# Seven-product steps in the mix and down products of a decoder block: one more in each, eleven premade sums, and activation sums made later

## The chip, the cores and the metric

One Trainium2 chip, one core. The metric is the device time of one execution in microseconds, the median of several runs. Times inside an execution come from a hardware profile of one run: its span, the busy time of each engine (PE is TensorE's matmuls, PEld its weight loads, DVE VectorE, ACT ScalarE, POOL GpSimd, SP SyncE), who waited for whom, and timelines.

## The reference

One decoder layer in float32 over 256 positions of width 2048. A large input projection, attention in three dilated groups and a gated recurrence end in gated branches y. Then, and this is the part that the change touches:

```python
h = h + rmsnorm(y @ w_mix_out[layer], norm_mix_post[layer])
a = rmsnorm(h, norm_ffn_pre[layer])
gt, up = jnp.split(a @ w_ffn_gate_up[layer], [D_FF], axis=-1)
ff = (jax.nn.silu(gt) * up) @ w_ffn_down[layer]
h = h + rmsnorm(ff, norm_ffn_post[layer])
```

`w_mix_out` is 2048 x 2048, `w_ffn_gate_up` 2048 x 11264, `w_ffn_down` 5632 x 2048. The weights are read once, 432 MB of traffic in all.

## The kernel before

**Split numbers.** Each float32 operand is split into a high part that TensorE multiplies exactly (ScalarE casts it, w or dh, L389 and L414) and the rest (VectorE subtracts, wl or dl, L409 and L417). A product takes three matmuls: high by high, high by low, low by high.

**Wide steps.** The large products run in blocks of 1024 output columns (two groups of 512), class `Wide`. A step takes 256 rows of the weight: two row blocks by two column groups, for two sides of 128 positions. By eight products that is 8 x 3 = 24 matmuls of 512 columns. By seven (in Strassen's manner) it is 21. For this a seven needs
- sums of the weight's four quarters (d, 128 x 1536; L399 to L404), split into dh and dl,
- one of them in the raw tile itself: after the raw load a DMA of GpSimd's queue adds the second row block onto the first (L302), so that the tile's high and low parts wait for it too,
- sums of the activations, split as well (so; `seven_sums`, from L543): in the mix by `pair_sums` (L555) in one of two lanes of side work, in the down product by `prep_act` within the step,
- four PSUM banks p1, p5, p6, p7, which after a block's last seven are gathered (L519 to L528) and then added to the four banks of the block's results (`add_up`, L533).

**Order of the work.** The instructions stand on each engine in program order. The main loop works two steps ahead: `ahead(n)` casts step n+2, makes its sums and its wl, and splits the sums of step n+1. There are three tiles for w, three for wl, one each for dh and dl. Three raw tiles (four from the FFN on): the load of step n+3 (n+4) waits until wl of step n is done. Where a block's last step is a seven, the gathering, `add_up` and only then wl of the step after next follow each other (`late`).

**The mix** is two blocks of eight steps, given by `MIX` as (row pair, by seven). In the first block, steps 3 and 5 are sevens, in the second, steps 2 and 4. The activations' sums of yT, pairs 0 and 1, are made in one go when pair 1 is there (`sums_of_y`, L1198). Beside its steps ScalarE's queue loads gains and x (gpost, hx, L1228 and L1235). Then `from_mix_to_ffn` interleaves the last steps, the norm and the first FFN steps by hand.

**The down product** is two blocks of 22 steps, `DOWN`; 8 steps of the first are sevens, and 9 of the second. The last three steps are run by side and column group, with the final norm behind them.

**Premade sums.** For steps listed in `READY` (by block and step: blocks 2 to 10 of the FFN, 11 and 12 for the two down blocks) the sums d are made ahead in DRAM, by six DMAs of GpSimd's queue each: three plain ones (L445), then, each on the one before, three accumulating ones (L449). Generators in `sums_before` are advanced once per step in the query-key-value stage, with `PACE` (4 steps between parts, 6 between starts). When a seven's sums are split, SyncE's queue loads the premade sums of the second next seven (`get_ready`, L423), in front of later raw loads. Such a step makes no additions for d.

Of the kernel before, what the change touches and what calls it, by code (L numbers as in the profile page):

```python
# [24 lines left out]
KF = FF // P  # L25
# [8 lines left out]
COL_GA, COL_GB = 13312, 15360  # L34

X7, H7 = tuple(range(4)), tuple(range(5))
MIX = [[(3, 0), (4, 0), (5, 0), (0, 1), (6, 0), (1, 1), (2, 0), (7, 0)],
       [(3, 0), (4, 0), (0, 1), (5, 0), (1, 1), (2, 0), (6, 0), (7, 0)]]

def order(steps):  # L40

    k = steps.count("7")
    return [(steps[:i].count(x) + k * (x == "8"), int(x == "7")) for i, x in enumerate(steps)]
# [1 line left out]

EARLY = [order(x) for x in ["88878878"] + ["87878787"] * 6 + ["88787878"]]
FFN = [order(x) for x in ["88878787"] + ["87877877", "87877877", "87877877", "87877877", "87877877", "87877877", "87877877", "87877877", "87877877"]]
DOWN = [[((n + 16 * j) % 22, n in by7) for n in range(KF // 2)] for j, by7 in enumerate( ([4, 6, 8, 10, 12, 14, 16, 18], [1, 3, 5, 7, 9, 11, 13, 15, 17]))]

TURN = 1  # L50
PAIRS = ((0, 0), (0, 1)), ((1, 0), (1, 1)), ("p1", "p6"), ("p5", "p7")
# [2 lines left out]


N_F = 16
READY, PACE, FIRST_READY, LAST_READY = {(2, 1), (2, 3), (3, 1), (3, 3), (4, 1), (4, 3), (5, 1), (5, 3), (6, 1), (6, 3), (7, 1), (7, 3), (8, 1), (8, 3), (9, 1), (9, 3), (10, 1), (10, 3), (11, 6), (11, 10), (11, 14), (12, 3), (12, 7), (12, 11), (12, 15)}, (4, 6), 2, 85


class Block:  # L60
# [48 lines left out]
def tile_hybrid_block(ctx: ExitStack, tc: tile.TileContext, t, out):  # L109
# [12 lines left out]
    def nm(s):  # L122
        serial[0] += 1
        return f"{s}_{serial[0]}"

    def rslot(s):
        return rpool.tile([P, 1024], F32R, tag="r", bufs=16, name=nm(s))
# [30 lines left out]
    def p3(s, dtype, n, bufs, tag=None):  # L158
        return pool["now"].tile([P, n], dtype, tag=tag or s, bufs=bufs, name=nm(s))
# [4 lines left out]
    def small(s, n=8, bufs=6):  # L164
        return cpool.tile([P, n], F32, tag=f"small{n}", bufs=bufs, name=nm(s))
# [65 lines left out]
    def ptile(s):  # L231
        n = {"early": 4, "middle": 5, "late": 2}[pool["name"]]
        return pool["now"].tile([P, 512], F32, tag="p", bufs=n, name=nm(s))
# [9 lines left out]
    blocks, seq, units, extra = [], [], [], []  # L243
# [11 lines left out]
    def add_seven(*args, flip, whole=True, stage=None, **kw):  # L255
        b = Wide(*args, **kw)
        b.flip, b.whole, b.unit0, b.stage = flip, whole, len(units), stage
        b.plus = stage == "ffn"
        blocks.append(b)
        for i in range(b.steps):  # L260
            seq.append(Step(b, i, len(units), 0))
            units.append([seq[-1]])
# [118 lines left out]
    def split_wide(st):  # L381

        b, raw = st.block, st.raw
        m, by7 = b.order[st.i]
        prep = b.prep(m, by7) if b.prep else iter(())
        next(prep, None)
        hi, lo = wslot(), wlow()
        st.parts = hi, lo
        nc.scalar.activation(hi, raw, AF.Copy)  # L389
        yield  # L390
        next(prep, None)
        if by7:
            w = raw.rearrange("p (n c) -> p n c", n=4)
            flat = st.sums
            if st.ready is None:
                flat = sums_slot(st)
                d = flat.rearrange("p (n c) -> p n c", n=3)
                if b.plus:
                    nc.vector.tensor_add(d[:, 0], w[:, 0], w[:, 2])  # L399
                    nc.vector.tensor_sub(d[:, 1], d[:, 0], w[:, 1])  # L400
                    nc.vector.tensor_add(d[:, 2], d[:, 0], w[:, 3])
                else:
                    nc.vector.tensor_sub(d[:, 0], w[:, 0], w[:, 2])
                    nc.vector.tensor_sub(  # L404
                        d[:, 1:], w[:, 1:4:2], d[:, 0:1].to_broadcast([P, 2, 512])
                    )
            st.rest = split_sums(st, flat, prep)
        yield
        nc.vector.tensor_sub(lo, raw, hi.bitcast(F32))  # L409

    def split_sums(st, flat, prep):

        hi, lo = (p3(x, F32R, 1536, 1) for x in ("dh", "dl"))
        nc.scalar.activation(hi, flat, AF.Copy)  # L414
        yield
        next(prep, None)
        nc.vector.tensor_sub(lo, flat, hi.bitcast(F32))  # L417
        st.parts += hi, lo
        later = [x for x in seq[st.n + 1 :] if type(x.block) is Wide and x.block.order[x.i][1]]
        if len(later) > 1 and later[1].ready is not None:  # L420
            get_ready(later[1])

    def get_ready(st):  # L423

        st.sums = sums_slot(st)
        nc.sync.dma_start(st.sums, st.ready)

    def sums_slot(st):
        n = [x for x in seq if x.block.__class__ is Wide and x.block.stage and x.block.order[x.i][1]]
        if len(H7) < 5 or st not in n:  # L430
            return p3("sum", F32, 1536, 1)
        return p3(("sum", "sum2")[n.index(st) % 2], F32, 1536, 1)
# [110 lines left out]
    def seven_sums(f, dst):  # L543

        s = ptile("s").rearrange("p (n t) -> p n t", n=4)
        x = f.rearrange("p k (s t) -> p (k s) t", s=2)
        nc.vector.tensor_sub(s[:, :2, :], x[:, 0:4:3, :], x[:, 1:2, :].to_broadcast([P, 2, P]))
        nc.vector.tensor_add(s[:, 2, :], s[:, 1, :], x[:, 0, :])
        nc.vector.tensor_sub(s[:, 3, :], x[:, 2, :], s[:, 2, :])
        yield  # L550
        nc.scalar.activation(dst[:, 0], s, AF.Copy)
        yield
        nc.vector.tensor_sub(dst[:, 1], s, dst[:, 0].bitcast(F32))

    def pair_sums(x, which, store, slot):  # L555

        for m in which:
            f = ptile("f").rearrange("p (k t) -> p k t", k=2)
            xs = x.slots[m]
            nc.vector.tensor_add(f, xs[:, :, 0, :].bitcast(F32), xs[:, :, 1, :].bitcast(F32))  # L560
            dst = slot().rearrange("p (z n t) -> p z n t", z=2, n=4)
            yield from seven_sums(f, dst)
            store[m] = sums_of(dst)
            yield

    def sums_of(dst):
        return lambda n: (dst[:, 0, n, :], dst[:, 1, n, :])
# [107 lines left out]
    evacs, turns, lanes, work, done = deque(), deque(), [deque(), deque()], deque(), []  # L675
# [16 lines left out]
    def flush(q):  # L692
        q = deque(q) if type(q) is list else q
        while q:
            advance(q)
# [477 lines left out]
    yT = []  # L1173
# [22 lines left out]
        return go  # L1196

    def sums_of_y():  # L1198
        while 1 not in yT[0].there:
            yield  # L1200
        yield from pair_sums(yT[0], (0, 1), y7, lambda: rslot("so"))


    zg, hx, gpost, zss = {}, {}, [], []
    h_t, hT, y7 = {}, [], {}
# [5 lines left out]
    def begin_mix():  # L1211
        flush(evacs)
        nc.scalar.preload_act_table_set("natural_log_exp_and_others")
        zss.append(small("zss"))

    def beside_mix(i):

        if i == 0:
            advance(turns)
        elif i == 1:  # L1220
            flush(turns)
        elif i < 4:
            j = i - 2
            if len(H7) > 4:
                gpost.append(p3("gpost", F32, (1024, 1536)[j], 1, ("act", "sum2")[j])[:, :1024])
            else:
                gpost.append(p3("gpost", F32, 1024, 3, "act"))
            nc.scalar.dma_start(  # L1228
                gpost[j],
                t["norm_mix_post"][:, j * 1024 : (j + 1) * 1024].to_broadcast([P, 1024]),  # L1230
            )
        else:
            j = i - 4
            hx[j] = p3("hx", F32, 1024, 4, "so").rearrange("p (b c) -> p b c", b=2)
            nc.scalar.dma_start(hx[j], xv[:, :, j * 512 : (j + 1) * 512])  # L1235
# [392 lines left out]
    for j in range(4):  # L1628
        add("N", t["w_attn_branch"][0], 8, 512 * j, heads, evac_attn_branch(j))
    blocks[-2].pre = lambda: lanes[1].append(sums_of_y())  # L1630
    blocks[-1].at[2] = begin_late
    for j in range(2):
        add_seven(t["w_mix_out"][0], (1024 * j, 1024 * j + 512), MIX[j],
                  lambda k: yT[0].after(turns)(k), lambda m: y7[m], evac_mix, flip=j == 0, whole=False,
                  pre=None if j else begin_mix, post=None if j else beside_mix)
    mix_end = len(seq) - 2
    mix_last = len(blocks) - 1
# [8 lines left out]
    for j in range(2):  # L1646
        add_seven(t["w_ffn_down"][0], (1024 * j, 1024 * j + 512), DOWN[j], act,
                  lambda m: a7[m], evac_down, stage="down", prep=prep_act, flip=j == 1, whole=j == 0,
# [3 lines left out]

    for n, st in enumerate(seq):
        st.n = n
    for j, b in enumerate(blocks[mix_last + 3 :], 1):
        b.plus = any(k == j for k, _ in READY)
    ready_in = range(blocks[10].unit0 + FIRST_READY, blocks[10].unit0 + LAST_READY)
    before = sums_before([
# [12 lines left out]
    later = []  # L1671
# [41 lines left out]
    for n, st in enumerate(seq):  # L1713
        b, i = st.block, st.i
# [49 lines left out]
    a, b, c = seq[-3:]  # L1764
# [61 lines left out]
```

## Time and profile before

| | us |
|---|---|
| runs before | 1686.75, 1684.83, 1686.53; median 1686.53 |
| the profiled execution | 1685.28 |
| its span | 1683.1 |
| TensorE busy | 1671.8 (99%) |
| VectorE busy | 1427.2 (85%) |
| ScalarE busy | 938.5 (56%) |
| mix, from the first to the last matmul of its 16 steps | about 900 to 985 |
| down product, 44 steps | about 1445 to 1674 |

The profile gives the span in forty slices, the groups of instructions by line and shape (count, busy time, mean duration, idle time in front of them and what ended it), who waited for whom, the chain of work that ended last, and timelines (start, duration, what; in brackets the idle time in front of it and its releaser). Matmuls are pipelined: they follow each other faster than the duration of one. TensorE's granted clock is full in nearly all slices.

### The profile page before, as it was taken

The numbers are of one execution on the slowest core, as the hardware profiler recorded it, in microseconds if no ns is written. First come the engines' busy times: TensorE is split into PE (matmuls) and PEld (weight loads), VectorE is DVE, ScalarE is ACT, GpSimd is POOL, SyncE is SP. The second block draws the span as 40 slices with busy tenths as digits, with TensorE's granted clock in tenths as the row PEclk, the third lists the DMA queues.
The fourth block names the chain that finished last, engine by engine and source line by source line (L and its number), as shares of the span: only waits on it lengthen the run. The fifth ranks groups of instructions, "written<-read, shape, count | busy, mean of one in ns | idle before, by whom it ended". The sixth has DMA issues, their size and how long they took to land.

```text
span 1683.1 us, 21771 instructions
## 1 busy us (share of the span) xinstructions
PE 1671.8 (99%) x8181; PEld 1402.6 (83%) x8181; DVE 1427.2 (85%) x1505; ACT 938.5 (56%) x962; POOL 225.2 (13%) x310
## 2 busy tenths in 40 slices
PE   9999999999999999999999999999999999999997
PEld 7888888888888888888888888888888888888886
DVE  6888898985887986777668887999999999899998
ACT  6655555554535434544445565566666666666763
POOL 0111111002320331321200010111111111000010
PEclk9999999999999999999999999999999999999999
DMA  8788888778995997995948857998998998888892
GB/s 280 264 264 253 260 260 257 244 244 290 319 265 175 318 292 232 303 313 177 291 150 250 269 174 253 276 273 273 277 273 271 277 287 265 263 256 253 242 301 99
DMA packets 241737, 432.63 MB, mean 257 GB/s; under 512 B 15168, under 2 KB 81776, under 8 KB 241632
## 3 DMA queue, kind: packets, MB, share of 16 engines
q1 hardware_dynamic: 201808, 337.55, 59.5%
q0 software_dynamic: 37200, 87.77, 22.5%
q10 hardware_dynamic: 2624, 5.92, 1.1%
q8 instruction: 64, 1.05, 0.3%
q14 instruction: 41, 0.34, 0.1%
HBM read 418.08 MB, written 52.43 MB: 280 GB/s over the span
## 4 chain that ended last, share of the span: by engine, by line
PE 94%; DVE 3%; issue 1%; DMA 1%; ACT 1%; SPq 0%; DVEq 0%; ACTq 0%
PE acc L168 59%; PE aux L168 34%; DVE wl L409 1%; DMA raw<-in_w_in 1%; PE aux L963 0%; PE acc L1451 0%; DVE dl L417 0%; PE aux L1451 0%; PE aux L632 0%; DVE e L537 0%; DVE w L355 0%; PE aux L620 0%; DVE e L528 0%; DVE fz L1573 0%; ACT w L354 0%
## 5 line engine op out<-in xcount | busy, mean ns | idle before, releaser
L389 ACT ACTIVATE w<-raw 128x2048 fp32r<-128x2048 f32 x204 | 390.2, 1913 | 220.8 <-issue 76.4
L409 DVE TENSOR_TENSOR wl<-raw,w 128x2048 fp32r<-128x2048 f32 x204 | 465.2, 2287 | 20.9 <-ACT w L389 19.0
L168 PE MATMUL acc<-xT,w 128*128 128x256 f32 (+1 forms) x2048 | 369.8, 339 | 0.0
L168 PEld LDWEIGHTS acc<-xT,w 128*128 128x128 f32 x2048 | 312.0, 188 | 43.8
L355 DVE TENSOR_TENSOR w<-raw,w 128x1024 fp32r<-128x1024 f32 (+1 forms) x191 | 232.5, 1218 | 135.4 <-ACT w L354 134.3
L354 ACT ACTIVATE w<-raw 128x1024 fp32r<-128x1024 f32 (+1 forms) x191 | 201.0, 1054 | 228.0 <-PE acc L168 184.3
L414 ACT ACTIVATE dh<-sum 128x1536 fp32r<-128x1536 f32 x98 | 146.1, 1491 | 141.9 <-PE aux L168 53.2
L417 DVE TENSOR_TENSOR dl<-sum,dh 128x1536 fp32r<-128x1536 f32 x98 | 171.9, 1754 | 19.3 <-ACT dh L414 18.9
L168 PE MATMUL acc<-w,xT 128*128 128x512 f32 x522 | 154.4, 392 | 0.3 <-DVE w L355 0.2
L168 PE MATMUL acc<-w,hT 128*128 128x512 f32 x504 | 152.8, 391 | 0.0
L168 PE MATMUL aux<-w,hT 128*128 128x512 f32 x368 | 122.8, 389 | 0.0
L168 PEld LDWEIGHTS acc<-w,xT 128*128 128x128 f32 x522 | 97.1, 188 | 21.6 <-DVE w L355 1.6
L168 PE MATMUL aux<-w,xT 128*128 128x512 f32 x346 | 111.9, 389 | 0.0
L168 PEld LDWEIGHTS acc<-w,hT 128*128 128x128 f32 x504 | 94.0, 188 | 19.7 <-DVE w L355 0.4
L302 POOL DMA_DIRECT2D raw<-in_w_ffn_gate_up x48 | 41.8, 871 | 378.2 <-DMA raw<-in_w_ffn_gate_up 179.4
L168 PE MATMUL aux<-w,a 128*128 128x512 f32 x258 | 82.6, 389 | 0.0
L168 PEld LDWEIGHTS aux<-w,hT 128*128 128x128 f32 x368 | 69.1, 188 | 14.3
L168 PE MATMUL acc<-w,a 128*128 128x512 f32 x242 | 77.4, 389 | 0.0
L168 PE MATMUL acc<-w,so 128*128 128x512 f32 x196 | 76.3, 389 | 0.0
L168 PE MATMUL aux<-w,so 128*128 128x512 f32 x196 | 76.3, 389 | 0.0
L168 PEld LDWEIGHTS aux<-w,xT 128*128 128x128 f32 x346 | 65.0, 188 | 13.4
L168 PE MATMUL aux<-dh,so 128*128 128x512 f32 x204 | 73.0, 392 | 0.0
(300 smaller groups left out, 2855.6 us busy)
## 6 DMA issues: line engine op xcount, KB each, us to landing
raw<-in_w_in SPq DMA_DIRECT2D x271, 512.0 KB, 6.2
raw<-in_w_ffn_gate_up SPq DMA_DIRECT2D x176, 512.0 KB, 5.1
raw<-in_w_ffn_down SPq DMA_DIRECT2D x88, 512.0 KB, 5.9
sum<-ready SPq DMA_DIRECT2D x25, 768.0 KB, 6.9
ready<-in_w_ffn_gate_up POOLq DMA_DIRECT2D x72, 256.0 KB, 6.7
raw<-in_w_mix_out SPq DMA_DIRECT2D x32, 512.0 KB, 5.6
ready<-ready POOLq DMA_DIRECT2D x50, 256.0 KB, 6.7
raw<-in_w_ffn_gate_up POOLq DMA_DIRECT2D x48, 256.0 KB, 6.4
```

Of the source, the lines that this page charges most:

```text
L168: nc.tensor.matmul(ps, lhsT, rhs, start=start, stop=stop, skip_group_check=True)
L302: nc.gpsimd.dma_start(raw[:, :512], rows, accum_op=OP.add)
L354: nc.scalar.activation(wh[:, k], raw[:, k], AF.Copy)
L355: nc.vector.tensor_sub(wl[:, k], raw[:, k], wh[:, k].bitcast(F32))
L389: nc.scalar.activation(hi, raw, AF.Copy)
L409: nc.vector.tensor_sub(lo, raw, hi.bitcast(F32))
L414: nc.scalar.activation(hi, flat, AF.Copy)
L417: nc.vector.tensor_sub(lo, flat, hi.bitcast(F32))
```

## The change

It makes step 7 of the first mix block a seven and orders pairs 7 and 2 anew; makes the activations' sums of pairs 0 and 1 separately, each as soon as its tile is there, and those of pair 2 when the mix begins; moves the down product's sevens (9 and 9 instead of 8 and 9, at even steps); lists 11 of them as premade instead of 7; starts a premade sum every 5 steps instead of 6. In `split_sums` a case for premade steps outside FFN and down is added, and `plus` is set over all blocks: no step of this plan comes under the first, and the second gives each block the value that it had.

```diff
-MIX = [[(3, 0), (4, 0), (5, 0), (0, 1), (6, 0), (1, 1), (2, 0), (7, 0)],
+MIX = [[(3, 0), (4, 0), (5, 0), (0, 1), (6, 0), (1, 1), (7, 0), (2, 1)],
        [(3, 0), (4, 0), (0, 1), (5, 0), (1, 1), (2, 0), (6, 0), (7, 0)]]
+Y7 = (0, 1, 2)
...
-DOWN = ... ([4, 6, 8, 10, 12, 14, 16, 18], [1, 3, 5, 7, 9, 11, 13, 15, 17]))]
+DOWN = ... ([4, 6, 8, 10, 12, 14, 16, 18, 20], [2, 4, 6, 8, 10, 12, 14, 16, 18]))]
...
-READY, PACE, ... (11, 6), (11, 10), (11, 14), (12, 3), (12, 7), (12, 11), (12, 15)}, (4, 6), 2, 85
+READY, PACE, ... (11, 6), (11, 10), (11, 14), (11, 18), (11, 20), (12, 4), (12, 8), (12, 12), (12, 14), (12, 16), (12, 18)}, (4, 5), 2, 90
...
-        if len(later) > 1 and later[1].ready is not None:
+        if later and later[0].ready is not None and not later[0].block.stage:
+            get_ready(later[0])
+        elif len(later) > 1 and later[1].ready is not None and later[1].block.stage:
             get_ready(later[1])
...
     def sums_of_y():
-        while 1 not in yT[0].there:
-            yield
-        yield from pair_sums(yT[0], (0, 1), y7, lambda: rslot("so"))
+        for m in Y7[:2]:
+            while m not in yT[0].there:
+                yield
+            yield from pair_sums(yT[0], (m,), y7, lambda: rslot("so"))
...
         zss.append(small("zss"))
+        lanes[1].append(pair_sums(yT[0], Y7[2:], y7, lambda: rslot("so")))
```

Three places show how instructions move. First VectorE at the end of the first mix block. In these rows wl is the low part of a step's weight, e the tile into which the seven-banks (aux) are gathered and to which the results (acc) are added, zg the gained output; the numbers are serial. Before:

```order
L409 TENSOR_TENSOR wl_7680<-raw_7566,w_7679 128x2048
L409 TENSOR_TENSOR wl_7714<-raw_7610,w_7713 128x2048
L526 TENSOR_TENSOR e_7742<-aux_7659,e_7742 128x512
L527 TENSOR_TENSOR e_7742<-aux_7663,e_7742 128x512
L528 TENSOR_TENSOR e_7742<-e_7742,aux_7667 128x1024
L409 TENSOR_TENSOR wl_7750<-raw_7646,w_7749 128x2048
L409 TENSOR_TENSOR wl_7783<-raw_7684,w_7782 128x2048
L541 TENSOR_TENSOR e_7742<-acc_7523,e_7742 128x512
```

The four wl are those of steps 6, 7, 8 and 9. The same place in the changed kernel, from the wl of step 6 on:

```order
L410 TENSOR_TENSOR wl_7718<-raw_7601,w_7717 128x2048
L404 TENSOR_TENSOR sum_7754<-raw_7646 128x512
L405 TENSOR_TENSOR sum_7754<-raw_7646,sum_7754 128x1024
L410 TENSOR_TENSOR wl_7752<-raw_7646,w_7751 128x2048
L418 TENSOR_TENSOR dl_7786<-sum_7754,dh_7785 128x1536
L410 TENSOR_TENSOR wl_7789<-raw_7684,w_7788 128x2048
L529 TENSOR_TENSOR e_7846<-aux_7697,e_7846 128x512
L530 TENSOR_TENSOR e_7846<-aux_7701,e_7846 128x512
L531 TENSOR_TENSOR e_7846<-e_7846,aux_7705 128x1024
L544 TENSOR_TENSOR e_7846<-acc_7552,e_7846 128x512
...
L410 TENSOR_TENSOR wl_7823<-raw_7722,w_7822 128x2048
```

(Three more additions are left out.) The sums and dl of step 7 are new, the gathering comes after wl of step 8, and wl of step 9 comes after the adding-up.

Second, GpSimd's queue in the query-key-value stage, in a stretch without other loads: rows of three transfers start a premade sum (`ready`), the single ones accumulate onto it. Before:

```order
L445 DMA ready_3687<-in_w_ffn_gate_up 128x512 x3
L449 DMA ready_3500<-ready_3500 128x512
L449 DMA ready_3687<-in_w_ffn_gate_up 128x512
L449 DMA ready_3500<-ready_3500 128x512
L445 DMA ready_3864<-in_w_ffn_gate_up 128x512 x3
```

and in the changed kernel:

```order
L448 DMA ready_3722<-in_w_ffn_gate_up 128x512 x3
L452 DMA ready_3416<-ready_3416 128x512
L452 DMA ready_3570<-ready_3570 128x512
L452 DMA ready_3722<-in_w_ffn_gate_up 128x512
L448 DMA ready_3870<-in_w_ffn_gate_up 128x512 x3
```

Two accumulations of the same sum stood on either side of one start; now each of the three rows between two starts belongs to another sum.

Third, VectorE between the two down blocks: a is an activation's low part, s the sums of activations, the additions of L537 are `add_up`. Before:

```order
L409 TENSOR_TENSOR wl_12437<-raw_12296,w_12436 128x2048
L601 TENSOR_TENSOR a_12468<-act_11072,a_12468 128x2x256
L547 TENSOR_TENSOR s_12475<-act_11072 128x256
L548 TENSOR_TENSOR s_12475<-s_12475,act_11072 128x128
L549 TENSOR_TENSOR s_12475<-act_11072,s_12475 128x128
L399 TENSOR_TENSOR sum_12480<-raw_12334 128x512
L400 TENSOR_TENSOR sum_12480<-sum_12480,raw_12334 128x512
L401 TENSOR_TENSOR sum_12480<-sum_12480,raw_12334 128x512
L409 TENSOR_TENSOR wl_12471<-raw_12334,w_12470 128x2048
L537 TENSOR_TENSOR e_12393<-aux_11644,e_12393 128x1024
```

and in the changed kernel:

```order
L527 TENSOR_TENSOR e_12513<-acc_11872,e_12513 128x512
L604 TENSOR_TENSOR a_12519<-act_11114,a_12519 128x2x256
L410 TENSOR_TENSOR wl_12522<-raw_12375,w_12521 128x2048
L540 TENSOR_TENSOR e_12513<-aux_11686,e_12513 128x1024
L540 TENSOR_TENSOR e_12513<-aux_11699,e_12513 128x1024
L1540 SCALAR_TENSOR_TENSOR fz_12562<-e_12513,r2c,fpost_11668 128x512
L1540 SCALAR_TENSOR_TENSOR fz_12566<-e_12513,r2c,fpost_11668 128x512
L604 TENSOR_TENSOR a_12555<-act_11414,a_12555 128x2x256
L550 TENSOR_TENSOR s_12570<-act_11414 128x256
L551 TENSOR_TENSOR s_12570<-s_12570,act_11414 128x128
L552 TENSOR_TENSOR s_12570<-act_11414,s_12570 128x128
L400 TENSOR_TENSOR sum_1879_12575<-raw_12415 128x512
```

The gathering's last row now stands two steps nearer to the adding-up, and the sums of the second block's first seven, which stood ahead of the adding-up, stand behind it.

More of the change, by code (lines that the diff above doesn't have):

```diff
@@ L47 @@
 FFN = [order(x) for x in ["88878787"] + ["87877877", "87877877", "87877877", "87877877", "87877877", "87877877", "87877877", "87877877", "87877877"]]
-DOWN = [[((n + 16 * j) % 22, n in by7) for n in range(KF // 2)] for j, by7 in enumerate( ([4, 6, 8, 10, 12, 14, 16, 18], [1, 3, 5, 7, 9, 11, 13, 15, 17]))]
+DOWN = [[((n + 16 * j) % 22, n in by7) for n in range(KF // 2)] for j, by7 in enumerate( ([4, 6, 8, 10, 12, 14, 16, 18, 20], [2, 4, 6, 8, 10, 12, 14, 16, 18]))]
 TURN = 1
@@ L56 @@
 N_F = 16
-READY, PACE, FIRST_READY, LAST_READY = {(2, 1), (2, 3), (3, 1), (3, 3), (4, 1), (4, 3), (5, 1), (5, 3), (6, 1), (6, 3), (7, 1), (7, 3), (8, 1), (8, 3), (9, 1), (9, 3), (10, 1), (10, 3), (11, 6), (11, 10), (11, 14), (12, 3), (12, 7), (12, 11), (12, 15)}, (4, 6), 2, 85
+READY, PACE, FIRST_READY, LAST_READY = {(2, 1), (2, 3), (3, 1), (3, 3), (4, 1), (4, 3), (5, 1), (5, 3), (6, 1), (6, 3), (7, 1), (7, 3), (8, 1), (8, 3), (9, 1), (9, 3), (10, 1), (10, 3), (11, 6), (11, 10), (11, 14), (11, 18), (11, 20), (12, 4), (12, 8), (12, 12), (12, 14), (12, 16), (12, 18)}, (4, 5), 2, 90
 class Block:
@@ L1654, in tile_hybrid_block @@
         st.n = n
-    for j, b in enumerate(blocks[mix_last + 3 :], 1):
+    for j, b in enumerate(blocks, -mix_last - 2):
         b.plus = any(k == j for k, _ in READY)
```

## The prediction

> **What bounds the kernel now.** I read the page's busy times first, then TensorE's own waits, then the timelines of the two stages that change.
>
> The page's head and TensorE's line, and the list of what TensorE waited for:
>
> ```profile
> span 1683.1 us, 21771 instructions
> PE 1671.8 (99%) x8181; PEld 1402.6 (83%) x8181; DVE 1427.2 (85%) x1505; ACT 938.5 (56%) x962; POOL 225.2 (13%) x310
> PE aux L168 <- DVE warm L210: 1.2, 1, 1.2
> PE aux L168 <- DVE wl L409: 0.6, 1, 0.6
> PE aux L168 <- DVE dl L417: 0.2, 1, 0.2
> PE acc L168 <- DVE w L355: 0.2, 1, 0.2
> ```
>
> TensorE waits for others 2.2 us in all. So the kernel is as long as its list of matmuls, plus a start and a tail. Only two things move the time: matmuls taken out, and new waits of TensorE. There is hardly a wait to win back.
>
> What a matmul costs is its spacing, not its duration of 0.39 us. TensorE's timeline at the first matmul of step 6 of the first mix block, and at the first one of the second block, 48 matmuls later:
>
> ```profile
> 932.00 0.39 PE L168 MATMUL acc<-w,yT 128*128 128x512 f32 x1
> 942.88 0.39 PE L168 MATMUL aux<-w,yT 128*128 128x512 f32 x1
> ```
>
> 10.88 / 48 = 0.2267 us. A step by eight products (24 matmuls) takes 5.44 us, one by seven (21) 4.76 us. I number the mix steps 0 to 7 in the first block, 8 to 15 in the second; step 7 begins at 932.00 + 5.44 = 937.44.
>
> **What is taken out.** One seven-product step more in the mix and one more in the down product (17 to 18): 2 x 3 x 0.2267 = 1.36 us. That is the whole possible gain, 0.08%; about 0.2% (3.4 us) is what a measurement of this kernel can tell from no change. The profiled execution took 1685.28 us, of which 1683.1 are the span; the median of the runs is 1686.53, 1.25 above it. The sum below is a difference, so I put it on the median.
>
> **The mix block: what step 7 now needs.** Groups by shape, with mean ns (VectorE, and ScalarE's cast of the sums):
>
> ```profile
> L409 DVE TENSOR_TENSOR wl<-raw,w 128x2048 fp32r<-128x2048 f32 x204 | 465.2, 2287 | 20.9 <-ACT w L389 19.0
> L417 DVE TENSOR_TENSOR dl<-sum,dh 128x1536 fp32r<-128x1536 f32 x98 | 171.9, 1754 | 19.3 <-ACT dh L414 18.9
> L404 DVE TENSOR_TENSOR sum<-raw,sum 128x1024 f32<-128x1024 f32 x36 | 44.1, 1225 | 1.2
> L403 DVE TENSOR_TENSOR sum<-raw 128x512 f32<-128x512 f32 x36 | 24.7, 687 | 22.2 <-DMA raw<-in_w_in 15.7 <-DMA raw<-in_w_mix_out 3.4 <-DMA raw<-in_w_ffn_gate_up 3.2
> L553 DVE TENSOR_TENSOR so<-s,so 128x512 fp32r<-128x512 f32 x28 | 19.2, 684 | 0.0
> ```
>
> Step 7 as a seven adds sums (0.69 + 1.23) and their low part (1.75): 3.7 us of VectorE, and moves the gathering of the seven-banks behind itself, directly ahead of the adding-up. It also needs an accumulating DMA from GpSimd's queue into its raw tile, which nothing of step 7 may read before. VectorE in this stretch, before:
>
> ```profile
> 903.46 2.28 DVE L409 TENSOR_TENSOR wl<-raw,w 128x2048 fp32r<-128x2048 f32 x1
> ...
> 915.56 2.29 DVE L409 TENSOR_TENSOR wl<-raw,w 128x2048 fp32r<-128x2048 f32 x1
> 918.07 0.69 DVE L403 TENSOR_TENSOR sum<-raw 128x512 f32<-128x512 f32 x1 [0.21 <-DMA raw<-in_w_mix_out]
> ...
> 929.44 2.29 DVE L409 TENSOR_TENSOR wl<-raw,w 128x2048 fp32r<-128x2048 f32 x1 [1.77 <-ACT w L389]
> 931.65 0.68 DVE L526 TENSOR_TENSOR e<-aux,e 128x512 f32<-128x512 f32 x1
> ...
> 934.37 2.28 DVE L409 TENSOR_TENSOR wl<-raw,w 128x2048 fp32r<-128x2048 f32 x1
> 939.59 2.29 DVE L409 TENSOR_TENSOR wl<-raw,w 128x2048 fp32r<-128x2048 f32 x1 [2.93 <-ACT w L389]
> 941.80 2.48 DVE L541 TENSOR_TENSOR e<-acc,e 128x512 f32<-128x512 f32 x4
> ...
> 946.72 0.69 DVE L403 TENSOR_TENSOR sum<-raw 128x512 f32<-128x512 f32 x1 [1.24 <-DMA raw<-in_w_mix_out]
> ...
> 952.02 1.76 DVE L417 TENSOR_TENSOR dl<-sum,dh 128x1536 fp32r<-128x1536 f32 x1 [0.32 <-ACT dh L414]
> ```
>
> With three raw tiles, the load of step n+3 starts when the low part (wl) of step n is done. From wl to a seven's first sum the rows give two prices: step 2's wl ends at 905.74 and step 5's sum starts at 918.07, 12.3 us; step 7's ends at 931.73 and step 10's sum starts at 946.72, 15.0 us. GpSimd's queue splits the first of them:
>
> ```profile
> 911.88 0.88 POOL L302 DMA_DIRECT2D raw<-in_w_mix_out  x1 [8.35 <-DMA raw<-in_w_mix_out]
> ```
>
> The accumulate is issued at 911.88, 6.1 us behind wl, and the sum starts 6.2 us after that. The Trainium skill prices such a transfer lower: "DMA: Bandwidth & Descriptors", section "Anatomy of one DMA — SWDGE (gpsimd) path", fits 2.0 us plus bytes over 436 GB/s, an estimate of 2.6 us for 256 KB and 3.2 for the 512 KB load, so that the sum of step 7 would come 5.8 us behind wl and nothing here would be late (1685.2 us). The trace shows twice that, and the trace decides.
>
> Step 4's wl ends at 917.85; it slips by about 0.7 us, since the low part of the third pair of activation sums (0.68) and ScalarE's cast for it now stand in this stretch. So step 7's sums start at 930.8 to 933.5. Sums, wl and dl follow each other: 1.9 + 2.3 + 1.8 = 6.0, so dl is done at 936.9 to 939.5. TensorE wants it at the fifth matmul of step 7 (products run 1, 6, 5, 7 there), 937.44 + 0.91 = 938.35. Late by nothing to 1.2; I take 0.6, since other loads (hx) fill the DMA engines just then, as they did for the 15.0.
>
> Then wl of step 8 (2.3, to 941.2), gathering (2.7 by the rows 931.65 to 934.37), adding-up (2.4), and only then wl of step 9 (2.3): done at 948.6. Before, it stood at 939.59. TensorE wants it at 937.44 + 4.76 + 0.6 + 5.44 + 0.23 = 948.5. Met by a hair: 0 to 0.3, I take 0.
>
> Step 10: its load starts behind step 7's wl, now 937.2 instead of 931.7, so its sums start at 949.5 to 952.2, and its wl is done 4.2 later, 953.7 to 956.4, against 953.9 wanted. Late by 0 to 2.5; I take 0.6. Step 12's load starts behind step 9's wl at 948.6, its sums 960.9 to 963.6, wl 965.1 to 967.8, wanted at 964.1 plus the delays so far: 0 to 1.2; by then the hx loads are over, I take 0.2. Behind it VectorE has the slack of the steps that follow, and the turn to the FFN shifts as a whole. What waits there is TensorE itself, with ScalarE's casts behind it, which wait for free operand tiles.
>
> Sum for the mix: minus 0.68, plus 1.4 (0 to 5).
>
> Making the first two activation sums apart (one when its tile is there, the other a step later) costs nothing: the same instructions, one step earlier, in a stretch where VectorE runs ahead of TensorE.
>
> **The down product.** Busy times in two stretches of 40 us (TensorE, its loads, VectorE, ScalarE, GpSimd, then clock, DMA share and GB/s), the second block's first matmul, VectorE about that boundary and near the end, and an addition of the sums:
>
> ```profile
> 1480.00:1520.00 40.00, 40.00 (x178) 33.14 (x177) 39.56 (x43) 26.68 (x25) 3.48 (x4) 1.00 0.88 267
> 1560.00:1600.00 40.00, 40.00 (x178) 33.13 (x177) 39.69 (x44) 27.72 (x29) 3.60 (x5) 1.00 0.81 244
> 1560.70 0.39 PE L168 MATMUL acc<-w,a 128*128 128x512 f32 x1
> 1559.90 2.35 DVE L537 TENSOR_TENSOR e<-aux,e 128x1024 f32<-128x1024 f32 x2
> ...
> 1569.22 0.69 DVE L601 TENSOR_TENSOR a<-act,a 128x512 fp32r<-128x512 f32 x1
> 1569.83 0.42 DVE L547 TENSOR_TENSOR s<-act 128x256 f32<-128x256 f32 x1
> ...
> 1570.82 2.28 DVE L409 TENSOR_TENSOR wl<-raw,w 128x2048 fp32r<-128x2048 f32 x1
> 1660.09 2.29 DVE L409 TENSOR_TENSOR wl<-raw,w 128x2048 fp32r<-128x2048 f32 x1 [0.67 <-ACT w L389]
> L399 DVE TENSOR_TENSOR sum<-raw 128x512 f32<-128x512 f32 x37 | 25.4, 685 | 1.6 <-DMA raw<-in_w_ffn_down 1.6
> ```
>
> VectorE is busy 39.6 of 40 us here and TensorE 40.0: VectorE keeps up by a few per cent. A seven without premade sums makes three additions like L399's, 2.06 us. Before, 17 sevens less 7 premade: 10 x 2.06 = 20.6. After, 18 less 11: 14.4. The extra seven adds dl (1.75) and the sums of its activations (1.0 from 1569.83 to 1570.82, and 0.68 for so). Net minus 2.7 us of VectorE, of which nothing reaches the time, as TensorE does not wait. The four more loads of premade sums (768 KB each) stand on SyncE's queue ahead of raw loads, as the seven do today.
>
> The boundary gets tighter. In the second block the first seven moves from step 1 to 2, so its sums now come behind the adding-up instead of ahead of it: adding-up 2.4 from 1560.0 (TensorE begins the block 0.7 ahead of 1560.70), three gains by fpost of 0.7, activations 1.6 (1569.22 to 1570.82), sums 2.1, wl 2.3, so and dl 2.4: dl at 1572.9, wanted ten matmuls into step 2, at 1560.0 + 10.9 + 2.3 = 1573.2. At the end the gathering (2.7) comes a step later, directly ahead of the wl at 1660.09, with 0.67 us of idle to fill. I take 0.1 (0 to 1). Down: minus 0.68 plus 0.1.
>
> **Premade sums ahead of time.** GpSimd's queue makes them in the query-key-value stage; it is paced by its own transfers. Two starts of one, a load that was blocked, the mix's first accumulate, a stretch, the landing of raw loads, and 48 matmuls of the stage:
>
> ```profile
> 445.19 1.90 POOL L445 DMA_DIRECT2D ready<-in_w_ffn_gate_up  x3
> 456.26 1.89 POOL L445 DMA_DIRECT2D ready<-in_w_ffn_gate_up  x3
> 526.22 0.77 POOL L800 DMA_DIRECT2D v<-kept  x1 [41.11 <-PE aux L168]
> 902.61 0.91 POOL L302 DMA_DIRECT2D raw<-in_w_mix_out  x1 [69.48 <-DVE gate L1190]
> 440.00:480.00 40.00, 40.00 (x240) 35.22 (x240) 36.88 (x50) 18.50 (x25) 15.64 (x23) 1.00 1.09 313
> DMA to landing us min/median/max: 3.7/9.5/14.0
> 498.55 8.43 PE acc L168 x48
> ```
>
> One takes 11.1 us of the queue; 29 instead of 25 are 44 us more, and the queue stands idle 41 us ahead of the first v and 69 us ahead of the mix. The new pacing overlaps three of them instead of two, which I reckon brings the 11.1 down to about 8. So the queue is in time; the price is a denser burst. I take 0.
>
> **Sum:** -1.36 + 1.4 + 0.1 = +0.1: 1686.6 us.
>
> **Rivals.**
> - *All slack holds.* Step 7's accumulate comes as fast as step 5's (12.3) or faster, and dl is there at 937. Then only the 1.36 are left: 1685.2. For it: the stretch before runs without a wait. Chance 0.34, beside 0.46 for the forecast.
> - *Slower: the burst starves the raw loads.* A 40 us stretch with a burst has DMA share 1.09 and 313 GB/s. A raw pair (1 MB) is wanted every 5.6 us (16 matmuls a step, 8.43 / 3 = 2.8 us), 187 GB/s. A load starts six steps, 16.9 us, ahead of its cast; the longest landing (stretch 680 to 760) is 14.0, and split tiles run one step or two ahead (2.8 each), so it decides at about 20 us. If raw loads got 5% less than they need in half the time from 445 to 833 (902.61 less 69.48), TensorE would lose 10: 1695. The same rows speak against it: no wait at 1.09. The skill's page on DMA, "Queues, rings and completion order", says that an engine takes its queues' packets in turn, which would take from the raw loads as GpSimd's queue fills; no row shows that share. Chance 0.08.
> - *Slower in the mix.* All the upper ends come true and the turn to the FFN, where VectorE's chain is dense, adds some: +5 to +6, 1691. Chance 0.08.
> - *VectorE was the hidden bound of the down product*, and its 2.7 us come back: 1682.5. Against it: 40.00 busy and 0.2 us of waiting. 0.03.
> - *Not what it says:* the premade sums aren't taken. The listing shows 11 loads in the down product. 0.01.
>
> Range: the first two cases with the scatter of the runs (1684.83 to 1686.75), and the mix's bounds up to +3: 1684.5 to 1689.5. Faster by over 0.2% 0.03, slower 0.13, the rest within.
>
> **What would show it.** Right: 8175 matmuls; TensorE waiting for wl or dl at step 7, 9, 10 or 12 of the mix, one to two us in all; the mix longer or even, the down product 0.7 shorter. Wrong: no such wait (1685.2), or casts (L354) waiting for raw loads between 400 and 850 us.

## The result, and the profile after

The change takes 1707.65 us (median of 6 runs, 1699.86 to 1711.24), the kernel before 1685.89 (6 runs, 1684.83 to 1686.75): a ratio of 1.0126, 95% interval 1.0112 to 1.0140. That is 21.8 us slower, far outside my range of 1684.5 to 1689.5. The rival to which I had given a chance of 0.08 came true: the denser making of premade sums starves the raw loads.

The head of the page, and, from the list of TensorE's waits (us in total, times, longest), the rows that bear on the argument:

```profile
span 1698.1 us, 21842 instructions
PE 1676.6 (99%) x8175; PEld 1404.5 (83%) x8175; DVE 1430.8 (84%) x1509; ACT 940.6 (55%) x966; POOL 244.7 (14%) x336
```

```profile
PE aux L169 <- DVE kk L1122: 2.8, 2, 1.9
PE acc L169 <- DVE w L356: 2.8, 4, 1.3
PE aux L169 <- DVE at L1049: 1.5, 1, 1.5
PE aux L169 <- DVE tot L1126: 0.9, 2, 0.5
PE aux L169 <- ACT pt L969: 0.9, 2, 0.7
PE aux L169 <- DVE wl L410: 0.8, 2, 0.6
PE acc L169 <- DVE dl L418: 0.3, 1, 0.3
```

The six matmuls are gone (8181 to 8175). New in the list are kk, at, tot and pt, and w has gone from 0.2 to 2.8: tiles of the query-key-value stage and its attention steps, not of the mix or the down product. To see how much each stage changed, I took from TensorE's timelines the start of the first matmul with wl and xT into an aux bank (56.88 before, 56.40 after), and of the first with recT, with yT, with hT and with a, and of the last one with a. These are the distances, of both traces and of those of all experiments (us; "branches" is from recT to yT):

| run | to branches | branches | mix | FFN | down |
|---|---|---|---|---|---|
| before | 742.97 | 99.78 | 85.81 | 460.13 | 228.46 |
| the change | 758.63 | 99.79 | 86.30 | 459.92 | 227.79 |
| after_again | 762.85 | 99.78 | 86.22 | 460.10 | 227.78 |
| b_pace45 | 762.65 | 99.78 | 85.81 | 459.85 | 228.47 |
| f_pace44 | 765.37 | 99.78 | 86.54 | 460.16 | 227.85 |
| i_pace43 | 780.83 | 99.78 | 85.81 | 459.87 | 228.46 |
| j_pace45_paused | 744.61 | 99.78 | 85.80 | 460.30 | 228.46 |
| a_pace46 | 743.72 | 99.78 | 88.81 | 460.48 | 227.78 |
| c_mix_only | 743.44 | 99.78 | 86.96 | 459.86 | 228.47 |
| d_down_25 | 743.43 | 99.78 | 85.80 | 459.94 | 231.17 |
| e_down_29_pace46 | 743.59 | 99.78 | 85.80 | 459.89 | 227.83 |
| e_again | 743.50 | 99.78 | 85.80 | 459.82 | 228.54 |
| g_mix_block1 | 743.40 | 99.78 | 86.28 | 460.11 | 229.58 |
| h_down_and_block1 | 742.94 | 99.77 | 86.58 | 460.51 | 228.13 |

The first column holds the whole loss: +15.66 us. The down product gains 0.67, the mix loses 0.49. The profiled execution of the change took 1699.86 us, the shortest of the six.

What the data transfers did in the first burst of premade sums, 410 to 480 us: packets, bytes and share by queue (q0 is GpSimd's: before, 37 premade transfers of 256 KB begin in the stretch, and its 9.44 MB are what 36 of them move; q1 carries the raw loads, 24 of 512 KB), and the median time to landing. The single row below each has the spread of the raw loads' landing. Before:

```profile
q0 software_dynamic: 4032, 9.44, 54.8%
q1 hardware_dynamic: 12789, 12.70, 53.4%
raw<-in_w_in SPq DMA_DIRECT2D x24, 512.0 KB, 8.7
ready<-in_w_ffn_gate_up POOLq DMA_DIRECT2D x25, 256.0 KB, 6.7
```

```profile
DMA to landing us min/median/max: 6.9/8.7/11.4
```

After, the same stretch:

```profile
q0 software_dynamic: 4784, 11.27, 62.9%
q1 hardware_dynamic: 10538, 10.47, 45.7%
raw<-in_w_in SPq DMA_DIRECT2D x20, 512.0 KB, 16.0
ready<-in_w_ffn_gate_up POOLq DMA_DIRECT2D x29, 256.0 KB, 6.9
```

```profile
DMA to landing us min/median/max: 6.7/16.0/20.6
```

Read the two queues against each other. Together they move nearly the same, 22.1 and 21.7 MB in 70 us, and their packets take the same share of the DMA engines, 108.2% and 108.6%: I read the engines as full in both. GpSimd's queue gains 1.83 MB, the raw loads lose 2.23 MB. The loss is the larger because a megabyte of premade transfers takes more of the engines' time than one of raw loads (54.8% for 9.44 MB against 53.4% for 12.70). A premade transfer lands about as fast as before (6.7 and 6.9 us); the raw loads alone pay, 16.0 us instead of 8.7.

How that reaches TensorE, in one place of the change's timeline:

```profile
467.59 1.06 ACT L355 ACTIVATE w<-raw 128x1024 fp32r<-128x1024 f32 x1 [1.69 <-DMA raw<-in_w_in]
468.69 1.23 DVE L356 TENSOR_TENSOR w<-raw,w 128x1024 fp32r<-128x1024 f32 x1 [1.02 <-ACT w L355]
470.47 0.68 DVE L1122 TENSOR_TENSOR kk<-kk,tot 128x512 f32<-128x512 f32 x1
471.21 2.96 PE L169 MATMUL aux<-q,kk 128*128 128x64 f32 x16 [1.92 <-DVE kk L1122]
```

ScalarE's cast waits for a raw tile, VectorE for the cast, and kk, which stands behind that on VectorE's queue, is late for TensorE. The name in TensorE's list (kk) is not the cause. Followed back, it shows in ScalarE's list, and it is the sign of being wrong that the prediction named (waits of the casts between 400 and 780 us; the first row is of before, where no raw load is in the list):

```profile
ACT w L354 <- PE acc L168: 131.4, 72, 3.5
```

```profile
ACT w L355 <- PE acc L169: 79.2, 47, 4.1
ACT w L355 <- DMA raw<-in_w_in: 78.6, 35, 4.6
```

Of the 15.66 us, TensorE's listed waits between 450 and 782 us make 9.2. Another 3.4 are a halved clock behind that wait for kk. Rows of 2 us each (TensorE, its loads, VectorE, ScalarE, GpSimd, then clock, DMA share, GB/s):

```profile
470.00:472.00 2.00, 0.79 (x7) 0.79 (x8) 2.00 (x5) 0.00 (x0) 0.83 (x1) 1.00 1.02 390
472.00:474.00 2.00, 2.00 (x12) 2.00 (x11) 2.00 (x3) 1.53 (x2) 1.37 (x2) 0.51 1.11 343
474.00:476.00 2.00, 2.00 (x8) 1.71 (x7) 2.00 (x3) 1.13 (x3) 0.00 (x0) 0.50 1.13 238
476.00:478.00 2.00, 2.00 (x8) 1.71 (x8) 1.97 (x6) 0.00 (x0) 1.10 (x3) 0.50 1.12 233
478.00:480.00 2.00, 2.00 (x11) 1.73 (x10) 0.62 (x2) 0.76 (x1) 0.90 (x2) 0.79 1.05 342
```

TensorE is busy all the time from 472 on, but at half the clock: 2 x (0.49 + 0.50 + 0.50 + 0.21) = 3.4 us lost. The other 3.1 us are in no listed wait, but most of them lie at the same places. Both traces have the same 3977 matmuls up to the branches; matched one by one, those behind the listed waits start 2.7 us later in all than the waits alone account for, 0.4 are one late start at 639.4 that the list leaves out, and 0.2 fall ahead of 450.

### The profile page after: what moved, and what is told of

The parts are those of the page before. It is cut to its first block, busy times and chain, and to the rows that moved or that the text cites. A ratio compares the mean times of both kernels' runs of the same rounds, so it can differ in the third digit from the quotient of the medians.

```text
span 1698.1 us, 21842 instructions
## 1 busy us (share of the span) xinstructions
PE 1676.6 (99%) x8175; PEld 1404.5 (83%) x8175; DVE 1430.8 (84%) x1509; ACT 940.6 (55%) x966; POOL 244.7 (14%) x336
## 4 chain that ended last, share of the span: by engine, by line
PE 76%; DMA 10%; DVE 8%; issue 3%; ACT 2%; SPq 0%; DVEq 0%; ACTq 0%; POOLq 0%
PE acc L169 47%; PE aux L169 27%; DMA raw<-in_w_in 9%; DVE wl L410 3%; DVE w L356 1%; ACT w L355 1%; DVE dl L418 1%; DVE e L540 1%; DMA raw<-in_w_mix_out 0%; DMA x<-in_x 0%; DVE sum L405 0%; DVE e L531 0%; ACT w L390 0%; DVE sum L404 0%; PE aux L966 0%
## 5 line engine op out<-in xcount | busy, mean ns | idle before, releaser
L418 DVE TENSOR_TENSOR dl<-sum,dh 128x1536 fp32r<-128x1536 f32 x100 | 175.4, 1754 | 21.2 <-ACT dh L415 20.9
L169 PE MATMUL aux<-w,a 128*128 128x512 f32 x244 | 78.6, 390 | 0.0
```

Of the source, the lines that this page charges most:

```text
L169: nc.tensor.matmul(ps, lhsT, rhs, start=start, stop=stop, skip_group_check=True)
```

## The experiments

My theory after the result: not the sevens and not the number of premade sums, but the one number that spaces them. With (4, 6) two sums are in progress on GpSimd's queue at a time, with (4, 5) three, and a sum is finished every 9.1 us instead of every 11.1. The change's starts show it: the first addition of a sum stands at 435.05, that of the third sum behind it at 462.48, 27.43 / 3 = 9.1.

```profile
435.05 0.81 POOL L452 DMA_DIRECT2D ready<-in_w_ffn_gate_up  x1 [0.66 <-issue]
462.48 0.80 POOL L452 DMA_DIRECT2D ready<-in_w_ffn_gate_up  x1 [0.67 <-issue]
```

The first rival: the four more sums, or the new sevens, cost it whatever the spacing.

**The spacing alone: b_pace45, a_pace46**

```
b_pace45, against before:
-READY, PACE, FIRST_READY, LAST_READY = {...}, (4, 6), 2, 85
+READY, PACE, FIRST_READY, LAST_READY = {...}, (4, 5), 2, 85
a_pace46, against the change:
-READY, PACE, FIRST_READY, LAST_READY = {...}, (4, 5), 2, 90
+READY, PACE, FIRST_READY, LAST_READY = {...}, (4, 6), -16, 88
```

Expected of b_pace45:

> The kernel before, with 25 premade sums and its old sevens, and one number changed: the next premade sum begins five steps behind the one ahead of it instead of six. Theory 1 (spacing): as slow as the change, 1700 to 1712, with raw loads landing in 14 to 18 us in the bursts and TensorE waiting for casts. Theory 2 (number): 1686, as before.

Measured: 1705.61 us (4 runs) beside 1685.43 of before, ratio 1.0118, interval 1.0101 to 1.0135. Its first burst reads like that of the change:

```profile
q0 software_dynamic: 4784, 11.27, 62.9%
q1 hardware_dynamic: 10527, 10.46, 45.7%
raw<-in_w_in SPq DMA_DIRECT2D x20, 512.0 KB, 16.2
```

Expected of a_pace46:

> The whole change with 29 premade sums, but each begun six steps behind the one ahead of it, as before, and the first of them 18 units earlier, so that all are done ahead of the mix. Theory 1 (spacing): the raw loads of the query-key-value stage were starved because a premade sum took 9 us instead of 11 of GpSimd's queue. Then no cast waits for a raw load here, raw loads land in 7 to 11 us in a burst, and the time is 1685.6 (1684.5 to 1687). Theory 2 (number): the four more sums, or the new sevens themselves, cost the time, whatever the spacing: 1700 or more.

Measured: 1688.42 us (11 runs), 1.0019 (1.0010 to 1.0028). The stage up to the branches is back at 743.72; the 3 us left are in the mix, below. One number moved by one gives nearly the whole slowdown to a kernel that has none of the rest, and taking it back (with an earlier first start) takes it away with all 29 sums kept. The number of sums is out.

**Rate, or three in progress: j_pace45_paused, i_pace43, f_pace44**

The spacing changes two things at once: how many sums are in progress, and how many bytes per time they move. j keeps three in progress and gives the old rate back:

```
j_pace45_paused, against before: (4, 6) becomes (4, 5), and
                 nc.gpsimd.dma_start(dst, src, accum_op=OP.add)
+            for _ in range(10):
+                nc.gpsimd.memset(idle, 0.0)
...
+        idle = p3("idle", F32, 128, 1)
f_pace44, against the change: (4, 5) becomes (4, 4)
i_pace43, against before: (4, 6) becomes (4, 3)
```

Expected of j_pace45_paused:

> The kernel before with the new spacing of five steps, so three premade sums in progress at a time as in the change, but behind each sum's last addition GpSimd clears a small idle tile ten times, some 2 us, ahead of the next accumulating transfer. Theory 1 (rate): what starves the raw loads is how much the premade transfers move per time; with a sum in about 11 us again (142 GB/s instead of 173) the raw loads land in 7 to 11 us and the time is 1686 (1685 to 1689). Rival (three in progress): transfers of three sums waiting side by side take the raw loads' turns whatever the rate: 1700 or more.

Measured: 1685.35 us (11 runs), 0.9999 (0.9990 to 1.0007). The ten clearings took 2.9 us rather than 2, and the pause brought the bytes back:

```profile
436.65 2.87 POOL L451 MEMSET idle<- 128x128 f32 x10
447.80 2.88 POOL L451 MEMSET idle<- 128x128 f32 x10
```

```profile
q0 software_dynamic: 4109, 9.69, 54.4%
q1 hardware_dynamic: 12777, 12.69, 53.7%
raw<-in_w_in SPq DMA_DIRECT2D x23, 512.0 KB, 10.6
```

Eleven microseconds from one sum's end to the next (436.65 to 447.80), 12.69 MB for the raw loads, and no loss in the median; the profiled execution is one of the longer ones (1686.55) and has 744.61 up to the branches. So it is the rate, not how many sums are in progress. What no run separates from the rate is how many premade transfers are under way at one moment: as each takes about the same time to land, the two rise together.

Expected of f_pace44:

> The whole change, with the premade sums yet denser: the next begins four steps behind the one ahead of it. Theory 1 (share of the DMA engines): a sum moves 6 x 256 KB, 142 GB/s at one in 11.1 us, 173 at one in 9.1, some 212 at one in 7.4; of the 313 GB/s of a burst 101 are left for the raw loads, which need 187. The shortfall grows from 12.4 MB to 18.5 over all bursts, worth 33 us more of TensorE: about 1740 (1720 to 1750). Rival (the premade transfers slow each other down): one sum still takes near 9 us, and the time stays at 1705 to 1715.

Measured: 1707.15 us (4 runs), 1.0125 (1.0110 to 1.0141). A miss: the instructions on GpSimd's queue are in the same order with four steps as with five (an addition comes every four steps, so a start one step later lands in the same gap). It is the change once more, with 11.19 and 10.52 MB in the burst, and says nothing on the dose. i puts four sums in progress:

Expected of i_pace43:

> The kernel before, with the next premade sum three steps behind the one ahead of it. The run with four steps put GpSimd's queue in the same order as five and so was no denser; three steps put four sums in progress. Theory 1 (rate): a sum in about 8 us, 197 GB/s, leaves 116 for the raw loads; the shortfall against 187 is 14.2 MB over 25 sums instead of 10.7 with five steps, where it costs 20 us; each MB more costs 5.3 us, so about 1724 (1712 to 1735). Rival (the premade transfers are themselves at their limit): a sum still takes 9 us, 1702 to 1710.

Measured: 1723.08 us (4 runs), 1.0219 (1.0205 to 1.0233).

```profile
q0 software_dynamic: 5188, 12.34, 67.8%
q1 hardware_dynamic: 9280, 9.22, 40.8%
raw<-in_w_in SPq DMA_DIRECT2D x16, 512.0 KB, 19.7
```

The time came as expected, though not by quite those terms: 12.34 MB in 70 us are 176 GB/s where I reckoned 197. The order of the doses stands without the model: 9.44 to 9.69 MB for GpSimd's queue in the burst cost nothing in that stage (before, a, j), 11.19 to 11.27 some 20 us (the change, b, f), 12.34 some 38.

**The same kernel again: after_again.** Expected:

> The change once more, unaltered, for a second profile: the first one took 1699.86 us and the five runs without a profile 1706 to 1711. If the loss is in the bursts, the stage from the first weight product to the branch products takes more than the 758.6 us of the first profile by as much as this run is longer, and mix, FFN and down product stay within 0.5 us of it.

Measured: 1705.27 us with the profile, 1708.85 without. This run was 5.4 longer than the first profiled one, of which 4.2 lie in the first column (762.85 against 758.63) and 1.1 ahead of it (57.48 against 56.40); the others agree within 0.2. The loss itself varies from run to run.

**The mix's third seven: c_mix_only, g_mix_block1**

```
c_mix_only, against before: the change's Y7, sums_of_y and begin_mix, and of MIX
-[[(3, 0), (4, 0), (5, 0), (0, 1), (6, 0), (1, 1), (2, 0), (7, 0)],
+[[(3, 0), (4, 0), (5, 0), (0, 1), (6, 0), (1, 1), (7, 0), (2, 1)],
g_mix_block1, against before: Y7, sums_of_y and begin_mix as in the change, and
-       [(3, 0), (4, 0), (0, 1), (5, 0), (1, 1), (2, 0), (6, 0), (7, 0)]]
+       [(3, 0), (4, 0), (0, 1), (5, 0), (1, 1), (2, 1), (6, 0), (7, 0)]]
```

Expected of c_mix_only:

> Of the change only the mix block: its third seven and the sums of its activations; the down product and the premade sums as before. Both theories: the mix takes 86.3 us instead of 85.8, as in the trace of the change, by waits for wl and dl late in the block, so 1686.4 (1685.5 to 1687.5). If the mix had more to do with the slowdown than the stage times show: 1690 or more.

Measured: 1686.79 us (11 runs), 1.0009 (1.0000 to 1.0017); the mix 86.96 instead of 85.81. GpSimd's accumulate for step 7, the sums behind it on VectorE, and TensorE's wait:

```profile
926.38 0.88 POOL L303 DMA_DIRECT2D raw<-in_w_mix_out  x1 [12.56 <-DVE dl L418]
933.88 0.69 DVE L404 TENSOR_TENSOR sum<-raw 128x512 f32<-128x512 f32 x1 [5.57 <-DMA raw<-in_w_mix_out]
938.11 1.75 DVE L418 TENSOR_TENSOR dl<-sum,dh 128x1536 fp32r<-128x1536 f32 x1
939.92 0.50 PE L169 MATMUL aux<-dl,so 128*128 128x512 f32 x1 [0.71 <-DVE dl L418]
```

The sums come 7.5 us behind the accumulate, and dl is done at 939.9.

Expected of g_mix_block1:

> Of the change only the mix's third seven, but in the second block instead of the first, at step 13, right behind the second seven of that block; all else as before. If the lateness comes from the place (the last step of a block, where gathering and adding-up follow at once and the hx loads fill the DMA engines), it goes, and the mix takes 85.1 us: 1684.8 (1684 to 1685.6). If it comes from the seven itself (its accumulating load and 3.7 us of VectorE more), the mix takes 86.3 to 87 wherever it stands: 1686 to 1687.5.

Measured: 1686.29 us (11 runs), 1.0004 (0.9995 to 1.0012); the mix 86.28. The wait has moved to the turn to the FFN:

```profile
984.58 0.50 PE L1293 MATMUL acc<-ident,h 128*128 128x128 f32 x2 [0.82 <-DVE h L1279]
```

By the stage times of these two traces the seven costs more than the three matmuls save in both places; by the medians c's interval just touches no change and g's includes it. That VectorE's 3.7 us more are what is late in g is likely from that row, not shown. In g's trace the down product, which this run leaves as it was, is 1.1 longer too (229.58), with 0.6 of waiting for wl near its end; whether the mix or chance did that, no run tells.

**The down product: d_down_25, e_down_29_pace46, e_again, h_down_and_block1**

```
all against before, with the change's DOWN and its get_ready rule:
d: READY with seven sums for the down product, at the new places, (4, 6), 2, 85
e, e_again: the change's READY with 29 sums, (4, 6), -20, 88
h: as e, and the mix of g
```

Expected of d_down_25:

> Of the change only the down product: 18 sevens at their new places, with 25 premade sums as before (seven of them for the down product), in the old spacing; the mix as before. Eleven sevens make their own sums. Three matmuls x 2 less, 0.7: 1685.2 (1684.5 to 1686.2) if VectorE keeps up without the four more premade sums; 1687 or more if it does not, and then the premade sums were needed.

Measured: 1688.21 us (11 runs), 1.0016 (1.0007 to 1.0025). The down product takes 231.17, 2.71 more than before; TensorE waits for wl near the end, the second time behind the gathering:

```profile
1661.24 0.50 PE L168 MATMUL acc<-wl,a 128*128 128x512 f32 x1 [0.41 <-DVE wl L409]
1666.83 0.50 PE L168 MATMUL acc<-wl,a 128*128 128x512 f32 x1 [1.20 <-DVE wl L409]
```

Expected of e_down_29_pace46:

> Of the change only the down product, with its 18 sevens and 29 premade sums, in the old spacing of six steps, the first sum 22 units earlier; the mix as before. If the four more sums are what the 18th seven and the sevens' new places need: the down product takes 227.8 us as in the trace of the change (231.2 with 25 sums), the rest as before, 1684.7 (1684.0 to 1685.6). If the four more sums cost time in the query-key-value stage or ahead of it even in the old spacing: 1686 or more.

Measured: 1684.41 us (11 runs, one of them at 2086.85) beside 1685.39 of before, 0.9992 (0.9983 to 1.0001); the down product 227.83.

Expected of e_again:

> The down product's part alone with 29 sums in the old spacing, once more, as its interval (0.9983 to 1.0001) did not tell it from no change: 1684.4 (1683.8 to 1685.2), ratio 0.9994, if the six matmuls saved are really all that differs.

Measured: 1684.49 us (11 runs) beside 1685.49, 0.9993 (0.9984 to 1.0002). Twice 1.0 us less; each interval just reaches no change. In its trace the down product took 228.54, with a wait of 0.5 for wl near the end, so that the margin there is thin.

Expected of h_down_and_block1:

> Down product with 18 sevens and 29 premade sums in the old spacing, and the mix's third seven in the second block: the two gains of 0.7 together if both hold, 1684.0 (1683.4 to 1685); 1685 to 1687 if one of them is lost.

Measured: 1686.04 us (11 runs), 1.0002 (0.9993 to 1.0011): the mix's seven takes back what the down product gained. The lowest median is e's: the down product's part of the change, with the premade sums started earlier instead of closer together.

## Why the prediction was wrong, step by step

- **What is taken out**: right. 8175 matmuls; the down product is 0.67 us shorter for the 0.68 forecast.
- **The mix**: right in mechanism, near in size. Forecast minus 0.68 plus 1.4, so 0.7 longer; measured 0.49 in the change's trace, 1.15 alone in c, 3.0 in a. In the change's own trace step 7 is on time (I took 0.6) and step 10 is late for wl and dl, 0.55 in all by the list (I took 0.6); 0.49 + 0.68 = 1.17 is the whole lateness, against the 1.4:

```profile
968.90 0.50 PE L169 MATMUL aux<-wl,yT 128*128 128x512 f32 x1 [0.20 <-DVE wl L410]
971.58 0.50 PE L169 MATMUL acc<-dl,so 128*128 128x512 f32 x1 [0.35 <-DVE dl L418]
```

  Which of steps 7 and 10 is late changes from trace to trace. Why a's mix is 1.85 longer than c's I did not settle; in a three of the last additions of premade sums stand between the mix's accumulates on GpSimd's queue (at 903.63, 914.08 and 929.03 us), where c and e have one, and no run singles that out.
- **The down product**: right, with 0 of the 0.1 of lateness. "Of which nothing reaches the time" was right for a gain, but d shows the other side: without the four more premade sums the same sevens lose 2.7 us, so VectorE is close behind TensorE there, and these sums carry the gain.
- **Premade sums: the step that failed.** I wrote "So the queue is in time; the price is a denser burst. I take 0". The queue was in time. The period was even milder than I reckoned, 9.1 us and not 8. But the term that I put at 0 measured 15.7 us in the change's trace, and the spacing alone (b) 20.2. What was wrong is how I read the row of 440 to 480 us: "no wait at 1.09" went down as evidence against starvation. A DMA share of 1.09 was not room left over: in the first burst both queues together moved 22.1, 21.7 and 21.6 MB (before, the change, i) while GpSimd's went from 9.44 to 11.27 and 12.34, so what one queue moved more the other moved less. Whether the engines or the memory behind them set that limit, no run tells. I set that share beside the raw loads' need of 187 GB/s but never took the one from the other: 313 GB/s in the burst less 142 (1.57 MB of a sum in 11.1 us) leaves 171 before, less 173 (in 9.1 us) leaves 140 after. The queues bear that out: between 440 and 480 us the raw loads' queue moved 7.05 MB before and 5.48 after, 176 and 137 GB/s. A shortfall of 16 was covered before (no wait), one of 47 was not. That the lead of the loads covers it within a burst, and the pauses between bursts give the lead back, is how I read it; no run singles it out.
- **The rival's price**: its point of decision, "about 20 us" to landing, fits (the longest in the first burst is 14.8 in the runs without the loss, a's, and 20.3 to 23.1 in those with it), its size does not: I took 5% less for the raw loads in half of the time and 10 us; they got 18% less in the first burst (10.47 for 12.70 MB), and the runs lost 21.8.
- **The rule of the Trainium skill** that spoke against the change pointed the right way: "DMA: Bandwidth & Descriptors", section "Queues, rings and completion order", has an engine take its queues' packets in turn. The runs agree as far as they can show it: the fuller GpSimd's queue, the less the other gets (12.70, 10.47, 9.22 MB), at nearly the same sum; that the turns go packet by packet no run shows. The prediction says that no row shows the share; the rows by queue of the 70 us above do.

## What to carry to other kernels

Where the DMA share of a stretch is as high as it gets in the kernel (1.08 to 1.09 over 70 us here), a stage without waits is not a stage with room: take each queue's bytes in that stretch, subtract, and compare what is left with what the waiting engine uses up. Work done ahead of time competes by its rate, not by its amount, so start it earlier rather than closer together. When a wait shows in a tile's name, follow it back along the queues of the engines: kk, at and pt were late here because a cast waited for a weight.

## What the runs showed of the hardware

A wait of TensorE can cost more than itself. Behind 1.92 us of waiting for kk the granted clock was 0.5 for some 6.8 us in the change's trace, with TensorE busy throughout. In i_pace43, with waits up to 3.1 us, four such stretches between 390 and 900 us add up to 13.7 us of 37.9 lost; before, a and j have none. Two rows of 4 us of i:

```profile
452.00:456.00 4.00, 2.12 (x5) 1.51 (x6) 2.36 (x2) 1.06 (x1) 2.23 (x5) 0.62 1.11 285
456.00:460.00 4.00, 4.00 (x15) 3.38 (x15) 2.52 (x5) 2.55 (x4) 1.57 (x2) 0.53 1.07 337
```

The Trainium skill, "TensorE: Matmul & The Clock Gate", section "What's actually happening", puts the halving behind an idle window of about 3.4 us. The trace agrees on the half rate; here it came with a longest single wait of 1.92 us, in a stretch of 6 us (466 to 472) in which TensorE was busy 60%.

The other surprise: in the same stretches at a DMA share of 1.08 to 1.09, the 256 KB loads of GpSimd's queue kept a median of 6.5 to 6.9 us to landing (before, the change, i), while the 512 KB loads of the other queue went from 8.7 to 16.0 and 19.7.
